# Layer 0's input projections of a two-layer decoder trunk, all with stationary activations and turned on TensorE afterwards

## The chip, the cores and the metric

The kernel runs on one core of a Trainium2 chip, in one launch. The metric is the device time in microseconds (us) from start to end of that core. Three runs of the kernel before gave 2135.3, 2136.2 and 2136.23 us; the median is 2136.2.

## What is computed

The trunk takes 256 tokens of 2048 features through two layers. Layer 0 is a recurrent mixer and a squared-ReLU MLP, layer 1 a dilated attention and an MLP. Only the mixer of layer 0 is touched by the change. Its reference, cut to what matters:

```python
def recurrent_mixers(h, w_in, ...):
    proj = h @ w_in                                   # (256 x 2048) @ (2048 x 6144)
    x_lru, y_lru, q_h, f_h, v_h, g_h = jnp.split(proj, list(IN_SPLITS), axis=-1)   # 1024 columns each
    lru = rg_lru(causal_depthwise_conv(x_lru, conv_w, conv_b), w_a, b_a, w_i, b_i, lam)
    lru = lru * jax.nn.gelu(y_lru.astype(F32), approximate=True)
    hg = hgrn2(q_h, f_h, v_h, g_h, lower_bound, g_norm)   # 8 heads of 128; RMSNorm per head, SiLU(g) gate
    mixed = jnp.concatenate([lru, hg], axis=-1).astype(h.dtype)
    return mixed @ w_out
```

The output of each head is divided by the root of its mean square over the head's 128 columns, multiplied by a gain per column, and by g times sigmoid(g). The recurrence and the convolution run along the tokens.

## The kernel before

**Number format.** Every large product is made from two rounded parts. An activation and a weight are each split into `hi` (the value rounded to float32r) and `lo` (the rest), and hi·hi, hi·lo and lo·hi are added up in PSUM. A weight tile of 128 x 2048 (1 MB, a *unit*) is fetched by SP into `raw`; ScalarE makes `hi` from it (line 130) and VectorE makes `lo` (line 131). The class `Weights` does both, in steps of 1024 columns for the units of layer 0's projections. `fetch` is called from `unit` and keeps two to three units ahead; `raw`, `hi` and `lo` have three buffers each.

**Two layouts of a projection.** In one, features come out on the partitions and tokens along the free dimension: the weights are the stationary operand of TensorE, the activations move. `project` (line 381) makes one block of 128 columns so, from one unit. With `cross` it issues 16 matmuls of 512 moving columns and 16 of 256; with `direct` 48 of 256. Heads 0 to 3 and `lru_in` of blocks 0 to 3 use `cross`; heads 4 to 7, `lru_in` of blocks 4 to 7 and all eight `lru_out` use `direct`. In the other layout tokens come out on the partitions: the activations are stationary and the weights move. `tokens` (line 348) makes 512 columns so from four units, 24 matmuls of 512 moving columns in each unit, in two PSUM banks, one for each half of the 256 tokens. Only the values v used this (`tokens_group`, line 373), in two groups of 512 columns.

**The row norm.** The activations in `bufa` are not normalised: the factor per token, `rt`, is applied after the projection. In the tokens layout it is a scale per partition, which the ACTIVATE that empties the bank takes along. In the features layout it is a row, so `over_tokens` (line 328) turns it once into `rs` and `scaled` (line 454) multiplies by it after each projection.

**A head.** `hgrn` (line 474) projects q and f, computes sigmoids, and then runs the scores in eight levels of doubling chunk size. In each level TensorE makes two small products of 64 columns from `qk` (line 509), VectorE copies masked results into `st` (line 512), and VectorE multiplies `qk` by a factor (line 526) before the next level's products. Three products with v give `po` (lines 533 to 535). The mean square and its inverse root are made for each head on its own (line 540 and `rsqrt`, 11 small VectorE operations); the two halves are scaled and turned to features (lines 544 and 547, `T.transpose`), the gate g is projected, and the product is split into `bufb` (block 8 + head).

**The other group.** `lru_in` projects a block of x, convolves it along the tokens and splits it into `bufb`. `lru_gates` multiplies four blocks by the gate weights (48 matmuls of 256) and computes sigmoids, then tanh and exp, then square roots, and runs the recurrence into `xc`. `lru_out` projects y, takes gelu, multiplies by `xc` and splits into `bufb` (blocks 0 to 7).

**Activation tables.** `lut` (line 251) keeps functions of one table together: whenever the kind changes (sigmoid; tanh and exp; square root), every later call is ordered behind all calls of the kind before.

**Order.** The string `ORDER` names the steps, and `units` follows it. Before, a head and a block of x alternate, v's second group comes in the middle, then gates 0, y 0 to 3, gates 1, y 4 to 7. After that `out_project` multiplies `bufb` by `w_out`: its first 512 columns take four units in the order `kgs` = (2, 3, 0, 1), which need blocks 8 to 11, 12 to 15, then blocks 0, 2, 4, 6 and at last 1, 3, 5, 7. All matmuls made through `mm` are chained in the order in which they are written. The small products of `hgrn` and the transposes are outside this chain: a scheduler puts each instruction into its engine's queue by priority, which is the place in the program moved ahead by `urgent` (400 instructions) or `stream` (150), and by when its operands are ready in the scheduler's own time model. On the chip each queue runs in that order.

`tokens` can run other work between its units: it takes the next entry of the list `steps` after each unit. Layer 1's attention uses this.

Of the kernel before, what the change touches and what calls it, by code (L numbers as in the profile page):

```python
# [10 lines left out]
F32 = mybir.dt.float32  # L11
# [30 lines left out]
def trunk_kernel(ctx, tc, head, x, xtok, cols, tab, masks, pos, fin, w_in, w_gate, w_out, w_qkv, w_o, w1, w2, out):  # L42
# [54 lines left out]
    where = {"x": (w_in, lambda i: i, 1), "y": (w_in, lambda i: 8 + i, 1), "g": (w_gate, lambda i: i, 1),  # L97
             "v": (w_in, lambda i: 14 + 16 * i, 4), "h": (w_in, lambda i: 18 + i // 4 * 16 + i % 4 * 3, 3)}
# [38 lines left out]
    def fetch():  # L137
        u = at[0]
        if u >= len(units):
            return  # L140
        at[0] += 1
        src, i = units[u][:2]
        with stream():
            if len(units[u]) > 2:
                combine(u, *units[u])
                return
            r = wraw.tile([P, 2048], F32, name="raw")
            loads[:] = [after(nc.sync.dma_start(r, src[i]), [])]
            made[u] = Weights(r, 1024)
# [107 lines left out]
    def cross(p, w, jobs, parts="hl"):  # L257
        for part in parts:
            for blk, mov, first, last in jobs:
                h, l = w.part(blk * P, P)  # L260
                if part == "h":
                    mm(p, h, mov, start=first, stop=False, skip_group_check=True)
                else:
                    mm(p[:, S:], l, mov[:, :S], start=False, stop=last, skip_group_check=True)

# [7 lines left out]

    PAIRWISE = 4
    of_head = lambda i: cross if i < PAIRWISE else direct
    YA = direct
# [51 lines left out]
    def over_tokens(r, turn=lambda o, i: T.transpose(o, i, ident)):  # L328
        p = psc.tile([P, 512], F32, name="pt", bufs=1)
        for j in range(2):  # L330
            turn(p[:, j * P:j * P + P], r[:, j:j + 1].to_broadcast([P, P]))
        return p[:, :S]

# [39 lines left out]
    def tokens_group(src, i0, rt=None, by_k=False, kgs=(0, 1, 2, 3), behind=()):  # L373
        ps = tokens(src, i0, bufa, kgs, by_k)
        v = vgs.tile([P, 2, 512], F32, name="vg")
# [5 lines left out]
    def project(src, i, mov, acc=None):  # L381
        w = unit(src, i)
        p = pmm.tile([P, 512], F32, name="p")
        jobs = [(k, mov[:, k], k == 0, k == KB - 1) for k in range(KB)]
        (acc or cross)(p, w, jobs)
        return p

# [7 lines left out]

    def square(j):
        q = wk.tile([P, 4, S], F32, name="gr", bufs=1).rearrange("p m s -> p (m s)").bitcast(BF16)
# [3 lines left out]
    vfirst = tokens_group(w_in, 14, by_k=True, behind=halfs[1:])  # L401
# [9 lines left out]
    rs = tmp.tile([P, S], F32, name="nr", bufs=1)  # L411
    A.copy(rs, over_tokens(rt))
# [41 lines left out]
    def scaled(p, z, acc=None):  # L454
        with urgent():
            if acc is direct:
                V.tensor_tensor(z, p[:, :S], rs, OP.mult)  # L457
            else:
                t = wk.tile([P, S], F32, name="t1", bufs=2)
                A.copy(t, p[:, S:])  # L460
                V.tensor_tensor(z, p[:, :S], t, OP.add)
                V.tensor_tensor(z, z, rs, OP.mult)

    def normed(p, name, bufs=2, acc=None):
        z = wk.tile([P, S], F32, name=name, bufs=bufs)
        scaled(p, z, acc)
        return z


# [4 lines left out]
    def hgrn(hd, vg):  # L474
        u0 = 18 + (hd // 4) * 16 + (hd % 4) * 3
        HA = of_head(hd)
# [3 lines left out]
        p = project(w_in, u0, bufa, HA)  # L480
        z = normed(p, "hz", 4, HA)
        lut(qp, z, AF.Sigmoid)
        V.scalar_tensor_tensor(qp, z, oml, qp, op0=OP.mult, op1=OP.mult)
        p = project(w_in, u0 + 1, bufa, HA)
        z = normed(p, "hz", 4, HA)
        f = wk.tile([P, S], F32, name="f", bufs=3)
        lut(f, z, AF.Sigmoid)
        lut(kq, z, AF.Sigmoid, scale=-1.0)
        V.tensor_scalar(f, f, oml, lb[:, hd:hd + 1], op0=OP.mult, op1=OP.add)
# [41 lines left out]
        vs = slice((hd % 4) * P, (hd % 4) * P + P)  # L531
# [4 lines left out]
        o = wk.tile([P, 2, P], F32, name="ho", bufs=2)  # L536
        hs = wk.tile([P, 2], F32, name="hs", bufs=2)
        for j in range(2):
            A.activation(o[:, j], po[:, j], AF.Square, accum_out=hs[:, j:j + 1])
        V.tensor_scalar(hs, hs, 1.0 / P, EPS, op0=OP.mult, op1=OP.add)  # L540
        hr = wk.tile([P, 2], F32, name="hr", bufs=2)
        rsqrt(hr, hs, 2)
        for j in range(2):
            A.activation(o[:, j], po[:, j], AF.Copy, scale=hr[:, j:j + 1])
        pt = psc.tile([P, 2, P], F32, name="pt", bufs=1)
        for j in range(2):
            T.transpose(pt[:, j], o[:, j], ident)
        p = project(w_in, u0 + 2, bufa, HA)
        z = normed(p, "hz", 4, HA)
        g = wk.tile([P, S], F32, name="g", bufs=2)  # L550
        lut(g, z, AF.Sigmoid)
        V.scalar_tensor_tensor(g, z, col("gn", hd), g, op0=OP.mult, op1=OP.mult)
        V.tensor_tensor(g, pt.rearrange("p j c -> p (j c)"), g, OP.mult)
        split_to(bufb[:, 8 + hd], g)
# [3 lines left out]
    def lru_in(b):  # L558
        XA = of_head(b)
        p = project(w_in, b, bufa, XA)  # L560
        xp = wk.tile([P, S + 4], F32, name="xp", bufs=1)
        V.memset(xp[:, :4], 0.0)
        scaled(p, xp[:, 4:], XA)
        A.activation(xc[:, b], xp[:, 4:], AF.Identity, bias=col("conv_b", b), scale=col("conv_w", 24 + b))
        for i in range(3):
            V.scalar_tensor_tensor(xc[:, b], xp[:, 1 + i:1 + i + S], col("conv_w", 8 * i + b), xc[:, b],
                                   op0=OP.mult, op1=OP.add)
        split_to(bufb[:, b], xc[:, b])

    def lru_gates(gp):  # L570
        w = unit(w_gate, gp)
        gr = wk.tile([P, 4, S], F32, name="gr", bufs=1)
        gi = wk.tile([P, 4, S], F32, name="gi", bufs=1)
# [21 lines left out]
    def lru_out(b):  # L595
        p = project(w_in, 8 + b, bufa, YA)
        y = tmp.tile([P, S], F32, name="z")
        scaled(p, y, YA)
        q = wk.tile([P, S], F32, name="q", bufs=1)
        A.activation(q, y, AF.Square, scale=math.sqrt(0.044715))  # L600
        V.scalar_tensor_tensor(q, q, 1.0, y, op0=OP.add, op1=OP.mult)
        lut(q, q, AF.Sigmoid, scale=2.0 * math.sqrt(2.0 / math.pi))
        V.tensor_tensor(y, y, q, OP.mult)
        V.tensor_tensor(y, y, xc[:, b], OP.mult)
# [627 lines left out]
```

## Time and profile before

| | us |
|---|---|
| median of three runs | 2136.2 |
| the profiled execution, its own time | 2134.95 |
| its span, first to last instruction | 2133.1 |
| of it, before `w_in`'s second step starts | 29 |
| the rest of layer 0's input projections and mixers | about 300 |
| `w_out` and all that follows | about 1804 |

In the profile PE is TensorE's matmuls, PEld its weight loads, DVE VectorE, ACT ScalarE, POOL GpSimd, SP the engine that issues most DMAs. A name such as `p<-bufa,hi` tells the tile that is written and those that are read. Views by line give a count, the busy time and the mean duration; a matmul's duration is that of one going through the pipeline, and since they overlap, what one costs in a row of many is read from the distance between starts in the timeline.

### The profile page before, as it was taken

What the parts mean: (1) busy time and instruction counts of PE and PEld (TensorE: products, weight loads), DVE (VectorE), ACT (ScalarE), POOL (GpSimd) and SP (SyncE); (2) the same over time, 40 slices, a digit from 0 to 9 for tenths busy, and PEclk for the clock granted to TensorE, in tenths of its full rate; (3) what the DMA queues carried; (4) which work ended last, traced back from release to release, by engine and by line L of the source; (5) the groups of instructions that cost most, each with busy time, mean ns of one, the idle gap of its engine ahead of it and who ended that gap; (6) DMA issues with size and microseconds to landing.
All of it is one profiled execution on the core that took longest, in us unless ns stands there. A gap on an engine that the chain in (4) does not pass through costs nothing.

```text
span 2133.1 us, 26563 instructions
## 1 busy us (share of the span) xinstructions
PE 2120.6 (99%) x10496; PEld 1796.1 (84%) x10496; DVE 1820.0 (85%) x1971; ACT 1306.2 (61%) x1394; POOL 72.3 (3%) x89
## 2 busy tenths in 40 slices
PE   9999999999999999999999999999999999999998
PEld 8889998888888888888888888888888888888887
DVE  7767789988888888889998888798988987988897
ACT  7444485666566566557665656566755655755764
POOL 0000000000000000000000000000000000000000
PEclk9999999999999999999999999999999999999999
DMA  8544446688878778877788667567888778787884
GB/s 328 175 171 144 156 155 224 217 256 257 253 232 272 251 242 246 275 243 236 239 271 249 207 215 219 215 211 242 238 241 282 236 247 262 251 254 238 275 260 156
DMA packets 69884, 498.13 MB, mean 234 GB/s; under 512 B 7808, under 2 KB 8064, under 8 KB 10240
## 3 DMA queue, kind: packets, MB, share of 16 engines
q1 hardware_dynamic: 57600, 410.90, 51.4%
q0 software_dynamic: 11872, 84.94, 21.3%
q8 instruction: 82, 1.34, 0.2%
q10 hardware_dynamic: 288, 0.61, 0.1%
q14 instruction: 42, 0.34, 0.0%
HBM read 494.31 MB, written 2.10 MB: 233 GB/s over the span
## 4 chain that ended last, share of the span: by engine, by line
PE 96%; DVE 2%; ACT 1%; DMA 1%; issue 0%; SPq 0%; DVEq 0%
PE p L221 61%; PE pd L221 15%; PE po L221 14%; PE pl L224 2%; PE pt L221 2%; PE pl L509 1%; DVE lo L131 1%; PE pl L221 1%; ACT hi L130 0%; DMA raw<-in_w_qkv 0%; DMA both_in<-in_head 0%; PE pd L493 0%; ACT bufa L284 0%; ACT L252 0%; DVE xc L593 0%
## 5 line engine op out<-in xcount | busy, mean ns | idle before, releaser
L130 ACT CAST hi<-raw 128x2048 fp32r<-128x2048 f32 (+1 forms) x408 | 663.4, 1641 | 505.1 <-PE p L221 304.1
L131 DVE TENSOR_TENSOR lo<-raw,hi 128x2048 fp32r<-128x2048 f32 (+1 forms) x408 | 793.9, 1954 | 181.1 <-ACT hi L130 175.1
L221 PE MATMUL p<-hi,bufa 128*128 128x512 f32 x1360 | 437.8, 392 | 0.6 <-ACT bufa L284 0.6
L221 PE MATMUL p<-hi,bufb 128*128 128x512 f32 x1264 | 404.4, 390 | 0.0
L221 PEld LDWEIGHTS p<-hi,bufa 128*128 128x128 f32 x1360 | 255.2, 188 | 53.7 <-ACT bufa L284 0.8
L131 DVE TENSOR_TENSOR lo<-s,hi 128x2048 fp32r<-128x2048 f32 x120 | 274.2, 2285 | 11.5 <-ACT hi L130 9.5
L221 PEld LDWEIGHTS p<-hi,bufb 128*128 128x128 f32 x1264 | 237.3, 188 | 48.9
L221 PE MATMUL p<-lo,bufa 128*128 128x512 f32 x680 | 265.4, 390 | 1.3 <-DVE lo L131 1.2
L130 ACT CAST hi<-s 128x2048 fp32r<-128x2048 f32 x120 | 229.6, 1913 | 52.0 <-PE po L221 23.1
L221 PE MATMUL p<-lo,bufb 128*128 128x512 f32 x632 | 245.9, 389 | 0.0
L221 PE MATMUL p<-bufa,hi 128*128 128x256 f32 (+1 forms) x1024 | 207.3, 313 | 0.1
L221 PEld LDWEIGHTS p<-bufa,hi 128*128 128x128 f32 x1024 | 166.6, 190 | 9.0 <-DVE hz L457 0.3
L221 PEld LDWEIGHTS p<-lo,bufa 128*128 128x128 f32 x680 | 127.7, 188 | 28.6 <-DVE lo L131 2.5
L221 PE MATMUL p<-bufa,lo 128*128 128x256 f32 x640 | 145.9, 286 | 0.0
L221 PEld LDWEIGHTS p<-lo,bufb 128*128 128x128 f32 x632 | 118.7, 188 | 24.4
L221 PE MATMUL pd<-hi,bufa 128*128 128x512 f32 x352 | 116.6, 393 | 0.0
L221 PE MATMUL p<-hi,formx 128*128 128x512 f32 x352 | 116.3, 391 | 0.0
L221 PEld LDWEIGHTS p<-bufa,lo 128*128 128x128 f32 x640 | 106.9, 191 | 1.3
L131 DVE TENSOR_TENSOR lo<-t,hi 128x2048 fp32r<-128x2048 f32 x40 | 91.5, 2288 | 16.5 <-ACT hi L130 16.5
L221 PE MATMUL po<-hi,bufb 128*128 128x512 f32 (+1 forms) x320 | 102.3, 386 | 0.0
L221 PE MATMUL p<-hi,formh 128*128 128x512 f32 x288 | 94.5, 389 | 0.0
L159 DVE TENSOR_TENSOR s<-s,raw 128x2048 f32<-128x2048 f32 x40 | 91.3, 2284 | 3.2 <-DMA raw<-in_w_qkv 3.1
(327 smaller groups left out, 3170.1 us busy)
## 6 DMA issues: line engine op xcount, KB each, us to landing
raw<-in_w SPq DMA_DIRECT2D x224, 1024.0 KB, 6.5
raw<-in_w_in SPq DMA_DIRECT2D x45, 1024.0 KB, 4.9
raw<-in_w_qkv SPq DMA_DIRECT2D x42, 1024.0 KB, 6.7
t<-in_w SPq DMA_DIRECT2D x32, 1024.0 KB, 6.6
t<-in_w POOLq DMA_DIRECT2D x32, 1024.0 KB, 8.8
s<-in_w POOLq DMA_DIRECT2D x32, 1024.0 KB, 8.7
raw<-in_w_out SPq DMA_DIRECT2D x15, 1024.0 KB, 4.9
raw<-in_w_o SPq DMA_DIRECT2D x15, 1024.0 KB, 4.9
```

What stands on the lines that cost most here:

```text
L130: casts[:] = [after(A.copy(h, w), [])]
L131: i = V.tensor_tensor(l, w, h.bitcast(F32), OP.subtract)
L159: return V.tensor_tensor(held[to], held[x], held[y], OP.add)
L221: chain[:] = [after(T.matmul(*args, **kw), chain)]
L224: chain[:] = [after(T.transpose(out_, in_, ident), chain)]
L509: T.matmul(pl[:, j], kq[:, js], halves(qp[:, js], c, True), start=True, stop=True)
```

## The change

All twelve groups of 512 columns of `w_in` now go through `tokens_group`. `project`, `cross`, `scaled`, `normed` and `over_tokens` are gone (`direct` stays for the gates), and so is the row `rs`; `rt` is applied by the ACTIVATE that empties each bank into a tile `tk` of 512 columns, of which there are seven buffers. Weights of `w_in` are laid out by groups and split in one step of 2048 columns.

Where features are needed on the partitions, the results are turned on TensorE: `turned` makes four 128 x 128 transposes into the one bank `pt`. A head turns its q and f; `lru_in` turns two blocks of x at a time and convolves straight from PSUM; `lru_out` turns two blocks of gelu(y) after `lru_gelu` has computed it on 512 columns; `finish` multiplies two heads' outputs by the inverse roots and by SiLU(g) with tokens on the partitions, turns them and splits them with the gain. The inverse roots are now made for four heads at once. One multiply-add of the forget gate moves from VectorE to ScalarE.

The order is new, and the heads and the other work are run between the units of later groups (`HOOKS`): a list of up to three entries for a group, one after each of its units. What is left after the last group, gelu and turning of y's second half, runs between the first two units of `w_out`, and the pool of the mixers is closed there too. The tiles of the gates, `gr` and `gi`, move into the room of `bufb`'s last quarter.

The diff, its core:

```diff
-    where = {"x": (w_in, lambda i: i, 1), "y": (w_in, lambda i: 8 + i, 1), ...
-    for step in ORDER.split():
-        src, first, n = where[step[0]]
-        units.extend((src, first(int(step[1])) + i) for i in range(n))
+    for g, step in enumerate(ORDER.split()):
+        if step[0] == "G":
+            units.append((w_gate, int(step[1])))
+        else:
+            units.extend((w_in, 4 * PLACE[step] + i) for i in range(4))
...
-            made[u] = Weights(r, 1024)
+            made[u] = Weights(r, 2048 if src is w_in else 1024)
...
+    def tokens_group(step, rt=None, by_k=False, behind=()):
+        steps[:] = HOOKS.get(step, ())
+        ps = tokens(w_in, 4 * PLACE[step], bufa, by_k=by_k)
+        v = vgs.tile([P, 2, 512], F32, name="tk", bufs=7)
...
+    def turned(tiles, at):
+        p = psc.tile([P, 2, S], F32, name="pt", bufs=1)
+        for i, (z, m) in enumerate(zip(tiles, at)):
+            for j in range(2):
+                T.transpose(p[:, i, j * P:j * P + P], z[:, j, m * P:m * P + P], ident)
+        return p
...
-        p = project(w_in, u0, bufa, HA)
-        z = normed(p, "hz", 4, HA)
-        lut(qp, z, AF.Sigmoid)
...
+        p = turned((done[f"q{g}"], done[f"f{g}"]), (at, at))
+        lut(qp, p[:, 0], AF.Sigmoid)
...
-        V.tensor_scalar(f, f, oml, lb[:, hd:hd + 1], op0=OP.mult, op1=OP.add)
+        A.activation(f, f, AF.Identity, scale=oml, bias=lb[:, hd:hd + 1])
...
+    def finish(g, half):
+        if not half:
+            hs = roots[g]
+            V.tensor_scalar(hs, hs, 1.0 / P, EPS, op0=OP.mult, op1=OP.add)
+            roots[g] = wk.tile([P, 8], F32, name="hr", bufs=2)
+            rsqrt(roots[g], hs, 8)
+        pair_ = [2 * half, 2 * half + 1]
+        for at in pair_:
+            o, z = outs[4 * g + at], done[f"g{g}"][:, :, at * P:at * P + P]
+            s = wk.tile([P, 2, P], F32, name="g", bufs=2)
+            lut(s, z, AF.Sigmoid)
+            V.tensor_tensor(s, s, z, OP.mult)
+            for j in range(2):
+                V.scalar_tensor_tensor(o[:, j], o[:, j], roots[g][:, 2 * at + j:2 * at + j + 1], s[:, j], ...)
+        p = turned([outs[4 * g + at] for at in pair_], (0, 0))
+        if g and not half:
+            bufb.tiles[3] = act.tile([P, 4, 2 * S], F32R, name="bufb3")
+        for i, at in enumerate(pair_):
+            split_to(bufb[:, 8 + 4 * g + at], p[:, i], col("gn", 4 * g + at))
...
+    def lru_gelu(n):
+        y = done[f"y{n}"]
+        q = outs[f"y{n}"] = vgs.tile([P, 2, 512], F32, name="tk", bufs=7)
+        for j in range(2):
+            A.activation(q[:, j], y[:, j], AF.Square, scale=math.sqrt(0.044715))
+            V.scalar_tensor_tensor(q[:, j], q[:, j], 1.0, y[:, j], op0=OP.add, op1=OP.mult)
+            lut(q[:, j], q[:, j], AF.Sigmoid, scale=2.0 * math.sqrt(2.0 / math.pi))
+            V.tensor_tensor(y[:, j], y[:, j], q[:, j], OP.mult)
+
+    def lru_out(n, half):
+        b0 = 4 * n + 2 * half
+        p = turned([done[f"y{n}"]] * 2, (2 * half, 2 * half + 1))
+        z = outs[f"y{n}"][:, half].rearrange("p (i s) -> p i s", i=2)
+        V.tensor_tensor(z, p, xc[:, b0:b0 + 2], OP.mult)
+        split_to(bufb[:, b0:b0 + 2], z)
+
+    HOOKS.update({
+        "q1": [head(0)], "f1": [head(1)], "v1": [head(2)], "x0": [head(3)],
+        "x1": [head(4), [do(lru_in, 0, 0)], [do(lru_in, 0, 1)]],
+        "g0": [head(5), [do(lru_in, 1, 0)], [do(lru_in, 1, 1)]],
+        "g1": [head(6), [do(finish, 0, 0)], [do(finish, 0, 1)]],
+        "y0": [head(7)],
+        "y1": [[do(lru_gelu, 0)], [do(lru_out, 0, 0), do(lru_out, 0, 1)], [do(finish, 1, 0)], [do(finish, 1, 1)]],
+    })
...
+    steps[:] = [[do(lru_gelu, 1)], [do(lru_out, 1, 0), do(lru_out, 1, 1), close_mixers]]
...
-ORDER = "v0 h0 x0 h1 x1 h2 x2 h3 x3 v1 h4 x4 h5 x5 h6 x6 h7 x7 g0 y0 y1 y2 y3 g1 y4 y5 y6 y7"
+ORDER = "v0 q0 f0 q1 f1 v1 x0 x1 G0 g0 g1 G1 y0 y1"
+PLACE = {step: n for n, step in enumerate(step for step in ORDER.split() if step[0] != "G")}
```

More of the change, by code (lines that the diff above doesn't have):

```diff
@@ L541, in hgrn @@
[L541 to L552, printed above, removed]
@@ L553, in hgrn @@
-        V.tensor_tensor(g, pt.rearrange("p j c -> p (j c)"), g, OP.mult)
-        split_to(bufb[:, 8 + hd], g)
-    xc = wk.tile([P, 8, S], F32, name="xc", bufs=1)
[L558 to L568, printed above, removed]
+            A.activation(o[:, j], po[:, j], AF.Square, accum_out=roots[g][:, 2 * at + j:2 * at + j + 1])
@@ L593, in lru_gates @@
             V.tensor_tensor_scan(xc[:, b], gr[:, m], xc[:, b], 0.0, op0=OP.mult, op1=OP.add)
[L595 to L604, printed above, removed]
-        split_to(bufb[:, b], y)
```

125 lines of the change are left out of this document (44 added, 81 removed).

## The prediction, made before the changed kernel was run

> **What bounds the kernel now.** I read the page first, then busy time by stage, then TensorE's groups of the first 460 us by shape, then the timeline.
>
> ```profile
> span 2133.1 us, 26563 instructions
> PE 2120.6 (99%) x10496; PEld 1796.1 (84%) x10496; DVE 1820.0 (85%) x1971; ACT 1306.2 (61%) x1394; POOL 72.3 (3%) x89
> ...
> PE 96%; DVE 2%; ACT 1%; DMA 1%; issue 0%; SPq 0%; DVEq 0%
> ```
>
> ```profile
> 29.00:135.00 106.00, 106.00 (x639) 94.43 (x638) 85.64 (x211) 57.64 (x103) 0.00 (x0) 1.00 0.57 201
> ...
> 160.00:329.00 169.00, 167.78 (x1411) 167.18 (x1411) 135.88 (x342) 101.41 (x202) 0.00 (x0) 1.00 0.43 150
> 329.00:350.00 21.00, 21.00 (x96) 17.39 (x95) 19.06 (x36) 11.32 (x17) 0.00 (x0) 1.00 0.75 270
> ```
>
> The chain that ended last is TensorE for 96% of the span. In the stages (columns: stretch, length, then busy time and count of PE, PEld, DVE, ACT, POOL, clock, DMA share, GB/s) it stays so in the part that the change touches, about 29 to 329 us: PE idles 1.22 us between 160 and 329, DVE is busy for 80% of each stretch, ACT for less, the DMA engines for half, and the granted clock is 1.00. What the change is worth is therefore what it takes from TensorE's queue, less what TensorE has to wait anew. Relief on DVE and ACT counts only where TensorE waits for them.
>
> **What a matmul costs in a row of many.** Starts in the timeline tell:
>
> ```profile
> 103.81 1.75 PE L221 MATMUL p<-bufa,hi 128*128 128x512 f32 x7
> 105.40 0.55 PE L509 MATMUL pl<-qk 128*128 128x64 f32 x4
> 105.77 1.18 PE L221 MATMUL p<-bufa,hi 128*128 128x512 f32 x4
> 106.78 2.06 PE L221 MATMUL p<-bufa,lo 128*128 128x256 f32 x16
> ```
>
> ```profile
> 205.26 0.40 PE L221 MATMUL p<-bufa,hi 128*128 128x256 f32 x2
> ...
> 208.49 0.40 PE L221 MATMUL p<-bufa,hi 128*128 128x256 f32 x2
> ```
>
> ```profile
> 330.95 0.62 PE L221 MATMUL p<-hi,bufb 128*128 128x512 f32 x2
> ...
> 337.75 0.62 PE L221 MATMUL p<-hi,bufb 128*128 128x512 f32 x2
> ```
>
> From 205.26 to 208.49 us lie nine groups of three matmuls of 256 columns: 3.23/27 = 0.1196 us each. From 330.95 to 337.75 lie ten groups of three of 512, in the tokens layout: 6.80/30 = 0.2267 us. The features layout costs the same for 512: 1.59/7 = 0.227 before the small products at 105.40. So twice the columns cost 1.90 times the time: each matmul carries some 12 ns beside its columns (2 x 0.1196 - 0.2267).
>
> **The main matmuls.** The counts:
>
> ```profile
> L221 PE MATMUL p<-bufa,lo 128*128 128x256 f32 x640 | 145.9, 286 | 0.0
> L221 PE MATMUL p<-bufa,hi 128*128 128x256 f32 x768 | 144.1, 287 | 0.1
> L221 PE MATMUL p<-bufa,hi 128*128 128x512 f32 x256 | 63.2, 394 | 0.0
> ```
>
> 768 = 24 `direct` units of 32, and 640 = 24 x 16 + 16 x 16 makes 16 `cross` units. A `direct` unit costs 48 x 0.1196 = 5.74 us, a `cross` unit 16 x (0.2267 + 0.1196) = 5.54, and a unit in the tokens layout 24 x 0.2267 = 5.44. The change saves 24 x 0.30 + 16 x 0.10 = **8.8 us**. v and the gates keep theirs.
>
> The Trainium skill, "TensorE: Matmul & The Clock Gate", section "Wait — 56ns, not 53.3ns?", speaks against so much: it gives about 2.5 ns of fixed cost to a matmul. By it the 24 x 24 + 16 x 8 = 704 matmuls that go would save 1.8 us, an estimate from that page, and the time below would be 7 us longer. The trace's own distances decide, so I keep 8.8 and give that rule no chance here.
>
> **The transposes.** A head, `finish`, `lru_in` and `lru_out` call `turned` 8 + 4 + 4 + 4 = 20 times, 80 transposes. These go:
>
> ```profile
> L547 PE MATMUL pt<-tab__183,ho 128*128 128x128 f32 x16 | 3.9, 272 | 0.0
> ...
> L328 PE MATMUL pt<-tab__183,nr 128*128 128x128 f32 x2 | 0.4, 272 | 0.0
> ```
>
> That leaves 62 more. Four transposes in a stream of 512s cost:
>
> ```profile
> 378.82 0.39 PE L221 MATMUL p<-hi,formh 128*128 128x512 f32 x1
> 379.05 0.60 PE L224 MATMUL pl<-tab__183,xall 128*128 128x128 f32 x4
> 379.41 0.48 PE L221 MATMUL p<-hi,bufb 128*128 128x512 f32 x1
> 379.72 0.40 PE L221 MATMUL p<-lo,bufb 128*128 128x512 f32 x1
> ```
>
> 378.82 to 379.72 is 0.90 us and holds two matmuls of 0.227, so four transposes cost 0.447 us, 0.112 each. The small products at 105.40 agree: 106.78 - 105.40 - 4 x 0.2267 = 0.47 for four. 62 x 0.112 = **6.9 us**. Low end: by columns alone, 12 ns and half of a 256's other 107, 0.066 us, the net is 80 x 0.066 - 18 x 0.066 = 4.1. High end: if none overlapped, 62 x 0.272 = 16.9. I take 6.9, because the row is this very operation among 512s. The heads' own small products (lines 493 to 535) stay as they are.
>
> TensorE's queue alone becomes 8.8 - 6.9 = **1.9 us shorter**.
>
> **What TensorE waits for anew.** DVE and ACT lose work: `scaled`, six of eight inverse roots, and a 2048-wide `lo` takes
>
> ```profile
> L131 DVE TENSOR_TENSOR lo<-raw,hi 128x2048 fp32r<-128x2048 f32 x67 | 153.4, 2289 | 37.9 <-ACT hi L130 37.8
> ...
> L804 DVE TENSOR_TENSOR y<-p,y 128x512 f32<-128x512 f32 x10 | 6.9, 688 | 4.0 <-PE p L221 4.0
> ```
>
> 2.29 us. They were hidden under TensorE, so this counts as nothing in mid-stage. In the opening a unit is now usable only after a whole 2048-wide cast and `lo`; its cover is the three units of `hi` and `lo`, and I charge nothing (up to 0.5). Three places are different, because a result that was spread over many units is now late by design.
>
> *`w_out`'s third unit.* It needs blocks 0, 2, 4, 6 in this order. Blocks 4 to 7 come from `lru_out`(1, ·), written behind `w_out`'s second unit, so its transposes stand in TensorE's queue behind that unit's matmuls and right ahead of the third's. Block 4 is wanted 6 x 0.2267 + 0.45 = 1.8 us later. Its path is transposes (0.45 and a pass of 0.27 less 0.11), a product from PSUM (0.69), a rounding on ACT (about the same), a difference on DVE (likewise): 2.7 us with every queue empty. The second half needs `pt` back, so it starts after the first's product and ends some 2 us later. With empty queues that stalls TensorE 0.6 to 1 us. They aren't empty: DVE was busy 19.06 of 21 us in this stretch, and the weights' casts and `lo`s, which run ahead by `stream`, and `mixed_forms` lie in between. Each of four DVE and two ACT steps can wait for a 1024-wide piece of about 1 us: 0 to 6 us, nothing if the scheduler found room for the transposes earlier. I take **4 us**, nearer to the top because DVE has 9% free.
>
> *`w_out`'s second unit* needs heads 4 to 7, and `finish`(1, 0) the roots of all four. Head 7 is written behind y0's first unit. In front of it stand the gates' square roots, since `lut` puts the head's sigmoids behind them:
>
> ```profile
> 307.84 0.47 ACT L252 ACTIVATE gi<-p,c__91 128x256 f32<-128x256 f32 x1
> ...
> 317.25 1.34 ACT L252 ACTIVATE gi<-gi 128x256 f32<-128x256 f32 x4
> ```
>
> From the last gate's sigmoid to the last root it took 10.8 us (with y's work on ACT between); y0's first unit covers 5.4, so the head starts up to 5 us late. A head takes, small products to `po`:
>
> ```profile
> 256.96 0.39 PE L493 MATMUL pd<-qk 128*128 128x128 f32 x2
> ...
> 294.53 0.39 PE L535 MATMUL po<-vg,st 128*128 128x128 f32 x2
> ```
>
> 38 us for head 7. With 3 us ahead of that and some 9 for `finish` (an estimate: twelve small DVE operations, products, transposes and splits, each behind a `lo`) it is ready 50 to 55 us after y0's first unit. TensorE gets there after eight units and some 60 small products: 43.5 + 6.7 = 50.2 us. 0 to 6 us, since a less busy DVE shortens the levels and the late start lengthens the whole; I take **2 us**, less than the middle for the emptier DVE. A stall here also gives the third unit's chain nothing, as that begins behind this unit.
>
> *Gates 0* want blocks 2 and 3 of x 5.4 + 24 x 0.1196 = 8.3 us after `lru_in`(0, 1) is written. Its path is transposes, two ACT steps, six convolution steps on DVE of about 0.5 us, a split: 5.6 us empty, up to 11 behind `lo`s and two heads. 0 to 3; I take **1 us**, as most of it fits.
>
> **The sum**: -8.8 + 6.9 + 4 + 2 + 1 = +5.1 us on the span of 2133.1. The median of the runs lies 3.1 above that span, so 2136.2 + 5.1 = **2141.3 us**.
>
> **The rivals.**
> *B, the covers hold.* The scheduler keeps TensorE's idle time as small as now (1.22 us), and only the queue counts: 2136.2 - 1.9 = 2134.3, not slower. For it: the same scheduler hid the tail of y before, with DVE just as full. Against: y's last block was wanted a unit later then, and no turn through TensorE stood in its path.
> *C, transposes don't overlap.* 16.9 in place of 6.9: 2151.3. The Trainium skill, same page, "Part 4: PE-mode transpose", gives about 275 ns to one in a kernel's context; its record here is 272, which agrees, but the distance between starts above is 0.112, and the clock stays at 1.00. Against it stand those rows; for it only that twenty bursts come in new company.
> *D, a head takes too long for its buffer.* The eighth `tk` tile is x1's, and it takes v0's room, which head 3 frees with `po`. Head 3 has seven units and 50 small products from where it is written, about 44 us. Head 2 took, with heads close together,
>
> ```profile
> 100.33 0.39 PE L493 MATMUL pd<-qk 128*128 128x128 f32 x2
> ...
> 164.08 0.39 PE L535 MATMUL po<-vg,st 128*128 128x128 f32 x2
> ```
>
> 64 us. From 44 us on x1's banks stay full and the gates stall: 20 us there, and again at `finish`: 2134.3 + 40 = 2174. Against: DVE was fuller, and a unit of v stood between.
> *E, cheap transposes and no waits.* 4.1 in place of 6.9, and the 1.22 idle gone: 2136.2 - 8.8 + 4.1 - 1.2 = 2130.3. For: a single transpose needs fewer columns. Against: the row of four.
>
> **How the numbers follow.** Forecast 0.45, B 0.27, C 0.06, D 0.09, E 0.13. 0.2% (4.3 us, 2131.9 to 2140.5) is about what a measurement can tell from no change. The forecast's own range is 2136 to 2149 (waits of 1 to 14 us); some 0.08 of its 0.45 lies within 0.2%. Faster: E, 0.13. Same: 0.27 + 0.08 = 0.35. Slower: 0.37 + 0.06 + 0.09 = 0.52. 2131 to 2150 leaves out D, C and half of E, 0.21.
>
> **What would show it.** Matmuls of 512 at 0.2267 us and four transposes at 0.45 show the queue; another distance breaks the first two terms. PE idle just ahead of `p<-hi,bufb` in `w_out`'s third unit, released by `bufb` on ACT or DVE, shows the 4; idle ahead of its second unit the 2; idle inside gates 0 the 1. If `w_out` starts about 2 us earlier than at 329.1 and runs without a gap, B holds and my waits are wrong. A bank of x1 emptied many us after its last matmul is D.

## The result, and the profile after

The changed kernel takes 2194.8 us (median of four runs, 2193.3 to 2196.2); the kernel before took 2136.2 on the same chip. The ratio is 1.0275, with a 95% interval of 1.0258 to 1.0293: 58.6 us slower, where the forecast was 5.1 slower and the range ended at 2150.

The page of the changed kernel, its span, busy times and granted clock:

```profile
span 2194.4 us, 25011 instructions
...
PE 2158.8 (98%) x9854; PEld 1784.0 (81%) x9854; DVE 1790.2 (82%) x1771; ACT 1312.4 (60%) x1337; POOL 72.5 (3%) x89
...
PEclk9999979999999999999999999999999999999999
```

642 matmuls and 200 VectorE instructions are gone, and yet TensorE is busy 38 us longer, and one slice of the clock row has a 7. The windows of the changed kernel (columns as in the prediction) tell where:

```profile
29.00:135.00 106.00, 106.00 (x494) 88.31 (x492) 57.25 (x86) 53.70 (x50) 0.00 (x0) 1.00 0.59 211
213.00:264.00 51.00, 51.00 (x258) 43.15 (x257) 42.75 (x91) 35.26 (x56) 0.00 (x0) 1.00 0.42 148
264.00:300.00 36.00, 22.98 (x96) 20.40 (x95) 15.07 (x42) 8.18 (x26) 0.00 (x0) 0.55 0.14 54
```

VectorE's share fell from 81% to 54% in the first stretch, as intended. From 264 to 300 us nothing is full: TensorE is busy for 23 of 36 us at a clock of 0.55, VectorE for 15, the DMA engines for a seventh. Everything waits for a chain there.

When `w_out`'s matmuls and all later ones are matched one by one in the two traces (7,724 of them), the changed kernel is 26.4 us late at the first, 46.1 after the 72nd (the end of `w_out`'s third unit), and then the lag grows evenly to 61.3 at the last. So there are three losses: before `w_out`, inside its first units, and a drift of 15 us over the untouched rest.

**The distances are those of the prediction.** TensorE in the changed kernel, four transposes between matmuls of 512:

```profile
126.18 0.39 PE L221 MATMUL p<-hi,bufa 128*128 128x512 f32 x1
126.41 0.60 PE L436 MATMUL pt<-tab__183,tk 128*128 128x128 f32 x4
...
127.31 0.63 PE L221 MATMUL p<-hi,bufa 128*128 128x512 f32 x2
...
129.36 0.61 PE L221 MATMUL p<-hi,bufa 128*128 128x512 f32 x2
```

From 126.18 to 127.31 lie three matmuls and four transposes: 1.13 - 3 x 0.227 = 0.45 us for the four. From 127.31 to 129.36 lie nine matmuls: 0.228 each.

**A head gets one level through per weight unit.** First TensorE's small products of one head (the two products of a level leave four records), then VectorE's queue at the same time (`lo` is the next unit's difference, lines 476 and 490 a level's copy and factor):

```profile
105.45 0.55 PE L473 MATMUL pl<-qk 128*128 128x64 f32 x4
111.83 0.55 PE L473 MATMUL pl<-qk 128*128 128x64 f32 x4
...
117.74 0.55 PE L473 MATMUL pl<-qk 128*128 128x64 f32 x4
124.11 0.55 PE L473 MATMUL pl<-qk 128*128 128x64 f32 x4
```

```profile
110.34 2.29 DVE L131 TENSOR_TENSOR lo<-raw,hi 128x2048 fp32r<-128x2048 f32 x1 [0.90 <-ACT hi L130]
112.55 0.29 DVE L476 COPY_PREDICATED st<-msk,pl 128x128 f32<-128x128 int8 x1
112.75 0.42 DVE L490 TENSOR_TENSOR qk<-qk,tot 128x256 f32<-128x256 f32 x1
...
116.71 2.29 DVE L131 TENSOR_TENSOR lo<-raw,hi 128x2048 fp32r<-128x2048 f32 x1 [2.88 <-ACT hi L130]
118.92 0.29 DVE L476 COPY_PREDICATED st<-msk,pl 128x128 f32<-128x128 int8 x1
```

The products of 111.83 us are copied at 112.55, as soon as `lo` lets VectorE go, and the factor is done at 113.17. The products of the next level come only at 117.74, 4.6 us later: in TensorE's queue they stand behind main matmuls, which follow each other without a gap. VectorE copies them at 118.92, behind the next unit's `lo`. Had the products come sooner, the copy would still have stood behind that `lo` in its queue, and the `lo` had waited 2.88 us, idle, for `hi`. ScalarE makes `hi` only when TensorE has freed a `hi` buffer, that is, once per unit; the cast had waited 4.45 us for that:

```profile
114.76 1.91 ACT L130 CAST hi<-raw 128x2048 fp32r<-128x2048 f32 x1 [4.45 <-PE p L221]
```

VectorE is not too full. Its queue and TensorE's each hold one level for each unit, and which of the two would give way first no run here separates. Eight levels at 6 us make a head of 44 to 50 us, and the heads go one after another: their `po` products come at 134.8, 178.6, 205.6, 240.6, 271.7, 285.8, 299.3 and 364.2 us, while the order writes a new one every 24 us.

**The backlog comes due at 264 us.** TensorE, once g1's matmuls are done:

```profile
277.05 1.08 PE L473 MATMUL pl<-qk 128*128 128x64 f32 x4 [0.88 <-DVE qk L490]
278.94 1.09 PE L473 MATMUL pl<-qk 128*128 128x64 f32 x4 [0.81 <-DVE qk L490]
...
299.89 0.64 PE L468 MATMUL pl<-qk 128*128 128x128 f32 x2
300.17 0.77 PE L221 MATMUL pl<-bufb,hi 128*128 128x256 f32 x2
```

With nothing else to do a level takes 1.9 us, at half the clock. Heads 4, 5 and 6 finish so, and the first matmul of gates 1, which writes a `pl` bank, follows head 6's last `pl` product at once.

**The tail.** TensorE in `w_out`'s second unit (first three rows) and third:

```profile
364.24 0.49 PE L497 MATMUL po<-tk,st 128*128 128x128 f32 x2 [1.11 <-ACT st L483]
369.54 1.26 PE L436 MATMUL pt<-tab__183,ho 128*128 128x128 f32 x4 [3.52 <-DVE ho L520]
371.37 0.79 PE L221 MATMUL p<-hi,bufb 128*128 128x512 f32 x1 [0.56 <-ACT bufb L271]
...
382.97 0.51 PE L221 MATMUL p<-hi,bufb 128*128 128x512 f32 x1 [0.34 <-ACT bufb L268]
385.10 0.74 PE L221 MATMUL p<-hi,bufb 128*128 128x512 f32 x2 [1.40 <-DVE bufb L269]
386.90 1.15 PE L221 MATMUL p<-hi,bufb 128*128 128x512 f32 x2 [0.83 <-DVE bufb L269]
```

Head 7 ends at 364 and its turn waits for `finish`; the second unit and its start lose 13 us. The third unit waits for blocks 4 to 7 just as foreseen.

**The drift.** The group of products with `formx`, of the kernel before and of the changed one:

```profile
L221 PE MATMUL p<-hi,formx 128*128 128x512 f32 x352 | 116.3, 391 | 0.0
```

```profile
L221 PE MATMUL p<-hi,formx 128*128 128x512 f32 x352 | 118.3, 397 | 0.0
```

The same instructions in layer 0's MLP and in layer 1, code that the change does not touch, take 6 ns longer, and the distance between the starts of two neighbours goes from 227.1 to 233.4 ns on the mean. Two things can be blamed: the two new 32 B temporaries of the inverse root for eight columns (`rs8`), which push `formx` and `formh` up by 64 B in SBUF, from 167456 and 200224 to 167520 and 200288; or another mix of traffic.

### The profile page after: what moved, and what is told of

The parts are those of the page before. It is cut to its first block, busy times and chain, and to the rows that moved or that the text cites. A ratio compares the mean times of both kernels' runs of the same rounds, so it can differ in the third digit from the quotient of the medians.

```text
span 2194.4 us, 25011 instructions
## 1 busy us (share of the span) xinstructions
PE 2158.8 (98%) x9854; PEld 1784.0 (81%) x9854; DVE 1790.2 (82%) x1771; ACT 1312.4 (60%) x1337; POOL 72.5 (3%) x89
## 4 chain that ended last, share of the span: by engine, by line
PE 96%; DVE 2%; ACT 1%; DMA 1%; issue 0%; SPq 0%; DVEq 0%
PE p L221 60%; PE pd L221 14%; PE po L221 14%; PE pl L224 2%; PE pt L221 2%; PE pl L473 1%; PE pl L221 1%; DVE lo L131 1%; ACT hi L130 0%; PE pt L436 0%; DMA raw<-in_w_qkv 0%; DMA both_in<-in_head 0%; PE po L497 0%; DVE qk L490 0%; PE pd L457 0%
## 5 line engine op out<-in xcount | busy, mean ns | idle before, releaser
L221 PE MATMUL p<-hi,bufa 128*128 128x512 f32 x2000 | 641.1, 393 | 0.8 <-ACT bufa L271 0.8
L221 PEld LDWEIGHTS p<-hi,bufa 128*128 128x128 f32 x2000 | 374.5, 188 | 78.6 <-ACT bufa L271 1.0
L221 PE MATMUL p<-hi,bufb 128*128 128x512 f32 x1264 | 409.7, 394 | 3.3 <-DVE bufb L269 2.2
L221 PE MATMUL p<-lo,bufa 128*128 128x512 f32 x1000 | 392.1, 392 | 1.3 <-DVE lo L131 1.3
L221 PEld LDWEIGHTS p<-lo,bufa 128*128 128x128 f32 x1000 | 187.9, 188 | 41.6 <-DVE lo L131 2.8
L159 DVE TENSOR_TENSOR s<-raw,t 128x2048 f32<-128x2048 f32 x40 | 91.3, 2283 | 0.4 <-DMA raw<-in_w_o 0.3
L221 PE MATMUL po<-hi,bufa 128*128 128x512 f32 x256 | 84.9, 392 | 0.0
L130 ACT CAST hi<-t 128x2048 fp32r<-128x2048 f32 x40 | 76.3, 1907 | 12.6 <-PE pd L221 6.4
L221 PE MATMUL pd<-hi,bufb 128*128 128x512 f32 x256 | 83.0, 389 | 0.0
```

Of the source, the lines that this page charges most:

```text
L130: casts[:] = [after(A.copy(h, w), [])]
L159: return V.tensor_tensor(held[to], held[x], held[y], OP.add)
L221: chain[:] = [after(T.matmul(*args, **kw), chain)]
```

## The experiments

Each was run beside the kernel before on the same chip; that one took 2135.3 to 2136.2 us. Labels with `a_` start from the changed kernel, with `b_` from the kernel before.

### Where formx and formh lie

```diff
  # in rsqrt: t = tmp.tile([P, n], F32, name=f"rs{n}", bufs=2)
  # a_pad
+ t = tmp.tile([P, 16 if n == 8 else n], F32, name=f"rs{n}", bufs=2)[:, :n]
  # a_fix
+ t = tmp.tile([P, 8], F32, name="rs2", bufs=2)[:, :n]
  # b_shift
+ t = tmp.tile([P, 16], F32, name=f"rs{n}", bufs=2)[:, :n]
  # b_512
+ t = tmp.tile([P, 72], F32, name=f"rs{n}", bufs=2)[:, :n]
  # b_480
+ t = tmp.tile([P, n], F32, name=f"rs{n}", bufs=17)
  # b_all0
  cst = pool("cst")
+ cst.tile([P, 120], F32, name="gap")
```

> The changed kernel with the two small tiles rs8 widened from 32 to 64 B, so that what is laid out behind them, formx and formh among it, moves by a further 64 B and comes to the place within 128 B that it had before the change. Nothing else differs. Address theory (a matmul whose stationary operand is formx or formh costs 233.5 ns in place of 226.6 because of the 64 B): those matmuls return to 226.6 ns and the time falls by some 15 us, to 2180. Rival (the longer distance comes from other engines' traffic or from the new order): no change, 2195.

> The kernel before with its two small tiles rs2 widened to 64 B each, which moves formx and formh by 64 B or a little more, and nothing else. Address theory: matmuls with formx or formh as the stationary operand go from 226.6 to about 233 ns and the time rises by some 15 us, to 2151. Rival (the order or the traffic): 2136, no change.

a_pad took 2194.6, no change. b_shift took 2150.0: the kernel before becomes 0.67% slower (0.52 to 0.82%) by a move of 64 B alone, and its row of `formx` shows the 397 ns of the changed kernel:

```profile
L221 PE MATMUL p<-hi,formx 128*128 128x512 f32 x352 | 118.3, 397 | 0.0
```

So the address does it, but not by its place within 128 B, which a_pad had restored in vain.

> The changed kernel with the eight-column temporaries of the inverse root under the name and in the two rooms of the two-column ones, so that formx and formh start at exactly the addresses that they had before the change (167456 and 200224). Address theory: those matmuls go back to 226.6 ns, and the time falls by some 15 us, to 2180, with the idle stretches of 200 to 390 us unchanged. Rival (the 64 B widening that had the same pitch of 233 was no test, since the place within 128 B is not what counts, and neither is the address): 2195, no change.

> The kernel before with formx and formh moved up by 512 B (167968 and 200736), by wider temporaries of the inverse root. 64 B up cost 14 us; in the changed kernel 128 B up of the old place cost the same as 64 B. If what counts is the place within 512 B, which is what one row of a 128-column operand takes: 226.6 ns a matmul and 2136. If it is the absolute place (a boundary above the old address): 233 ns and 2150.

a_fix took 2179.4, 15.4 less than the changed kernel: the drift is gone (43.9 us late after `w_out`'s third unit, 44.1 at the last matmul). b_512 (a single run, as b_480 and b_all0 below) took 2135.0, with the old duration:

```profile
L221 PE MATMUL p<-hi,formx 128*128 128x512 f32 x352 | 116.3, 391 | 0.0
```

> The kernel before with formx and formh moved by 480 B to 167936 and 200704, which are multiples of 512; so far places of 32 B past a multiple of 512 cost 226.6 ns a matmul and places of 96 and 160 B past it 233.5. If 32 B or less past it is harmless: 2135 and 226.6 ns. If only the offset that the other buffers share (32 B) is: 2150 and 233 ns.

> The kernel before with one gap of 480 B ahead of everything, so that all big tiles (activations, hi and lo of the weights, formx, formh) start at multiples of 512 instead of 32 B past one. In the kernel before all of them stand 32 B past a multiple of 512; moving formx and formh alone to a multiple of 512 cost 12 us. If what counts is that the stationary operand and the moving one (hi, lo) stand at the same place within 512 B: 2135, all at 226.6 ns. If 32 B is good by itself and 0 is bad: all of some 7700 matmuls of 512 columns take 6.8 ns more, 2185.

Moved alone to a multiple of 512, the two tiles are slow again, 2147.9 us (b_480); with every large tile at a multiple of 512 they are fast, 2136.3 us (b_all0). Rows of b_480 and of b_all0, where one more line of code makes line 221 line 222:

```profile
L221 PE MATMUL p<-hi,formx 128*128 128x512 f32 x352 | 118.0, 396 | 0.0
```

```profile
L222 PE MATMUL p<-hi,formx 128*128 128x512 f32 x352 | 116.3, 391 | 0.0
```

No place is good or bad by itself. A product is fast where its stationary tile stands at the same offset within 512 B as the other large tiles (32 B in the kernel before, 0 in b_all0). Its moving operand, `hi` or `lo`, is the natural partner, but the runs moved all other tiles together and do not single it out.

### What holds the heads

```diff
  # a_nopl: gates 1
- p = psc.tile([P, 512], F32, name="pl", bufs=2) if gp and not gate else pmm.tile([P, 512], F32, name="p")
+ p = pmm.tile([P, 512], F32, name="p")
  # a_half: in hgrn, behind a level's copies
+ if c == 8:
+     c = 128
+     continue
  # a_1024
- made[u] = Weights(r, 2048 if src is w_in else 1024)
+ made[u] = Weights(r, 1024)
```

> The changed kernel, but the second gates unit takes only pmm banks and never the pl bank that the heads' levels use. Theory that the pl bank holds it back (its first matmul waits for every earlier head's levels): the matmuls of gates 1 start right behind g1's last one, near 264 us, and TensorE's idle 264 to 300 us goes from there; but the heads' backlog stays and shows again ahead of w_out's second unit, so of the 24 us lost there only 0 to 12 are won: 2183 to 2195. Rival (gates 1 waits for another thing, its input blocks or a pmm bank): no change, 2195, and the idle stays where it is.

2184.3 us. The windows of a_nopl:

```profile
250.00:300.00 50.00, 49.95 (x277) 43.20 (x276) 41.59 (x95) 37.92 (x64) 0.00 (x0) 1.00 0.47 165
300.00:355.00 55.00, 45.10 (x212) 37.99 (x210) 30.26 (x54) 21.47 (x47) 0.00 (x0) 0.81 0.34 119
```

The idle stretch of 264 to 300 us is gone, gates 1 start at 264.5 right behind g1, and `w_out` starts at 322.9, 6 us before the kernel before. But the backlog waits behind it: heads 6 and 7 end at 338 and 351 us, `w_out`'s second unit stands for them, and of a stretch of 36 us only 10.5 are won. The `pl` bank decided where the backlog fell due, not that there was one.

> Each head leaves out its levels of 16, 32 and 64 columns: scores between blocks of those sizes and their factors are missing from the output. Backlog theory (a head gets about one level through per weight unit, because DVE serves each level behind the next unit's lo, so that the heads take 44 us each where a group supplies one every 24): heads end some 16 us sooner each, the idle of TensorE at 264 to 300 us vanishes and so does most of that at 361 to 390 us; 24 small products of 3 levels x 2 x 8 = 48 go besides, about 4 us. The time falls by 30 to 45 us, to 2150 to 2165. Rival (the idle is set by the gates' own chain and by lru_out, not by the heads): only the products go, 2188 to 2192.

2167.0 us: 28 less, where 30 to 45 were expected. The heads' `po` come at 117, 142, 168, 192, 207, 260, 273 and 330 us, and `w_out` starts at 327.5. Not all of the 28 is backlog: the records of the small products fall from 224 to 128, 24 levels of four, and at the 0.47 us for four that the prediction read they alone are worth up to 11 us, not the 4 that were expected. The rival, corrected by that, would have stood at 2184, still far from the result. What is left, besides the address's 15, are waits that have little to do with levels: 2.0 us at gates 0 for blocks of x, 3.0 ahead of head 6's first products for a sigmoid, and 4.6 ahead of the turn of head 7's outputs.

> The changed kernel with the input weights split in two casts and two lo of 1024 columns each, as before the change, and not in one of 2048. Theory that a level waits because DVE's queue alternates levels and units: the queue still has one level for each unit, so no change within 4 us of 2195. Rival (the 2.29 us lo of 2048 columns is what a level waits for): levels fit between the two pieces, heads go twice as fast, and 20 to 30 us go: 2165 to 2175.

2188.6 us, 6 less than the changed kernel: two us outside what the first theory gave, and far from its rival. VectorE's queue still has one level for each unit (copies at 105.49, 111.48 and 117.84 us, each behind its pair of `lo`). The width of the split is not what a level waits for.

### Two levels per unit

Each head becomes a generator that yields after a level, and two heads take turns. Both versions have a_fix's temporaries and a_nopl's banks.

```diff
+            yield                          # in hgrn, at the end of a level
+    def pair_of(h):
+        live = [hgrn(h), hgrn(h + 1)]
+        while live:
+            for f in list(live):
+                if next(f, live) is live:
+                    live.remove(f)
  # a_levels
-        "q1": [head(0)], "f1": [head(1)], "v1": [head(2)], "x0": [head(3)],
+        "q1": [[heads(0)]], "v1": [[heads(2)]], "x0": [[], [], [], [heads(4)]],
...
+        "g1": [[do(finish, 0, 0)], [do(finish, 0, 1)], [heads(6)]],
  # a_pairs
-ORDER = "v0 q0 f0 q1 f1 v1 x0 x1 G0 g0 g1 G1 y0 y1"
+ORDER = "v0 q0 f0 q1 f1 v1 x0 x1 g0 G0 g1 G1 y0 y1"
+        "g0": [[do(lru_in, 1, 0)], [do(lru_in, 1, 1)], [heads(6)]],
```

> The changed kernel at the old addresses (2179.4) with heads written in pairs, level by level in turn, and gates 1 in the pmm banks only; its order of groups and its gates stay. Heads 6 and 7 are written behind finish of the first four. Theory that one level per unit made the backlog: heads 0 to 5 end 30 to 60 us earlier than in the changed kernel, the idle of 264 to 300 us goes, that at the end stays for the late heads 6 and 7: 2155 to 2168. Rival (the gates and their own chain hold up TensorE there): 2175 to 2180.

2156.2 us. TensorE's small products in a_levels:

```profile
106.05 1.00 PE L473 MATMUL pl<-qk 128*128 128x64 f32 x8
111.95 1.00 PE L473 MATMUL pl<-qk 128*128 128x64 f32 x8
```

The pace is the same 6 us, now for two levels. Heads 0 to 5 end at 137, 150, 191, 203, 225 and 238 us in place of up to 286; heads 1, 3, 4 and 5 gain 29 to 48 us, head 2 gains 15 and head 0 nothing, so "30 to 60" was too much for some. `w_out` starts at 326.4, and the late heads 6 and 7 cost 24 us behind it, as expected.

> The changed kernel with its heads written in pairs, level by level in turn, so that two levels stand between one weight unit's lo and the next instead of one; heads 6 and 7 before finish (with eight ho tiles, and fewer f and g tiles for the room), gates 0 behind g0, gates 1 in the pmm banks only, and formx and formh at their old addresses. Nothing is left out. Theory that one level per unit made the backlog: heads end 44 us a pair, TensorE's idle before w_out falls from some 30 us to under 4, the clock stays at 1.00, w_out starts at 326 to 330 us, and with 0 to 8 us at the tail the time is 2132 to 2142. Rival (the heads are slow because DVE and ACT are too full, however they are written): two levels take two units, the idle stays, 2165 to 2180.

2153.1 us: between the theories. The heads are out of the way (the last `po` at 316 us), but `w_out` starts at 336.6. Gates 0, moved behind g0, now run into gates 1: gates 1 write into the room that gates 0's scans still read, and TensorE idles some 7 us between 265 and 284. And 8.6 us go in `w_out`'s second and third units, where heads are late no more: this is the tail that the prediction charged with 2 + 4.

### The order

The pairs of heads, `lru_in`, `finish` and `lru_out` are hooked in behind the units that finish their inputs, some units ahead of their use; q0 is now the first group, so that heads start four units earlier, and gates have other groups between them.

```diff
  # a_order
+ORDER = "q0 f0 v0 x0 q1 G0 f1 v1 x1 g0 G1 y0 y1 g1"
-    units.extend((w_out, 4 * n + g) for n in range(2) for g in (2, 3, 0, 1))
+    units.extend((w_out, 4 * n + g) for n in range(2) for g in range(4))
  # a_order2
+ORDER = "q0 f0 v0 x0 q1 f1 G0 v1 x1 g0 y0 G1 y1 g1"
+    with urgent():
+        finish(1, 0)
+        finish(1, 1)
  # a_order3
+ORDER = "q0 f0 v0 x0 q1 f1 G0 v1 x1 g0 y0 y1 G1 g1"
  # a_order4: as a_order2, but
-        "g0": [[go(6, 5), do(lru_in, 1, 0)], [do(lru_in, 1, 1)], [], [do(root, 0)]],
+        "g0": [[do(lru_in, 1, 0), go(6, 5)], [do(lru_in, 1, 1)], [], [do(root, 0)]],
```

> All of it put together, nothing left out: groups in the order q0 f0 v0 x0 q1 G0 f1 v1 x1 g0 G1 y0 y1 g1, heads in pairs level by level, gates 1 in the pmm banks, old addresses, and w_out's units in the order 0 1 2 3, so that the blocks of lru_out and finish are each wanted several units after they are written. Theory that the change itself is worth its shorter queue (1.9 us) once the waits that came with its order are gone: TensorE's idle up to the end of w_out's first 512 columns is under 4 us, the clock is 1.00, and the time is 2132 to 2140. Rival (the gates' chains on ACT and DVE find no room beside the heads whatever the order): 2145 to 2155, as with the pairs alone.

> As the version with the new order (2145.2), nothing left out, with these moves: each pair of heads is written some units earlier, G0 behind f1 and G1 behind y0, the inverse roots ahead of finish, finish of the last four ahead of w_out, and its second half and that of lru_out turned through a pl bank instead of waiting for pt. Theory that only the order's waits keep the change from its 1.9 us: the waits at gates 0 (1.6 us), gates 1 (3.4) and in w_out's last unit (5) fall to 0 to 4 together, 2134 to 2140. Rival (each wait taken away comes back one step further): 2142 to 2148.

> As the second version with the new order (2139.4), but gates 1 behind y1 instead of y0, so that the last pair of heads has its levels behind it when gates 1 begin; nothing left out. TensorE lost some 4 us there (small products one at a time and a stretch at a lower clock at 272 to 280 us). Theory: that goes, and lru_out of blocks 4 to 7 has one unit of cover less before w_out, 0 to 2 us: 2134 to 2138. Rival (it comes back ahead of w_out): 2139 to 2142.

> As the second version with the new order (2139.4), but the first block pair of lru_in for gates 1 written ahead of the last pair of heads; nothing left out. Theory: gates 1 have their input blocks earlier and the heads' last levels fall among the matmuls behind them: 2134 to 2138. Rival (the heads are then later for w_out's last unit): 2139 to 2144.

2145.2, 2139.4, 2137.4 and 2136.4 us. a_order lost 9 us at gates 0, gates 1 and in `w_out`'s last unit; a_order2 lost 4 at gates 1 alone; the last two have no wait of note left up to the end of `w_out`. a_order4 against the kernel before: 1.0004, interval 0.9995 to 1.0013, a tie, with 2135.3 beside it. No version beats the kernel before. The windows of a_order4:

```profile
160.00:327.00 167.00, 166.59 (x881) 142.43 (x880) 120.79 (x228) 105.82 (x177) 0.00 (x0) 1.00 0.46 160
327.00:350.00 23.00, 23.00 (x107) 18.99 (x106) 19.58 (x38) 13.67 (x22) 0.00 (x0) 1.00 0.61 224
```

TensorE is full at full clock. `w_out` starts at 326.4, 2.7 us before the kernel before, and from its third unit up to 1075 us the lead is an even 1.8. Then it is given back in layer 1. The longest waits of VectorE for a transfer between 1115 and 1145 us in the kernel before, and between 1125 and 1145 in a_order4:

```profile
DVE s L159 <- DMA raw<-in_w_qkv: 1.6, 1, 1.6
```

```profile
DVE s L159 <- DMA raw<-in_w_qkv: 3.1, 1, 3.1
```

A weight of layer 1 lands late there in both; TensorE waits for its `lo` 1.0 and 2.5 us, and in a_order4 the clock falls to 0.91 in that window. Why it is longer there stays open: TensorE waited 2.4 to 2.8 us at this place in a_half, a_levels, a_order2 and a_order3 too, some of which came there later than the kernel before and some sooner, and 0.9 to 1.4 in all other versions.

## Why the prediction was wrong, and where it was right

Taken against the kernel before of each run, the 58.6 us come apart so: the address 15.3 (changed kernel to a_fix), levels and bank 22.7 (a_fix to a_levels), order 19.5 (a_levels to a_order4), and 1.1 left. No run has the heads in turn without the change of the bank, so the 22.7 stay together.

**Main matmuls -8.8 and transposes +6.9: right in kind.** Both distances were measured again (0.228 and 0.45 for four), and in a_order4, where the waits are gone, the lead is 1.8 us where 1.9 was forecast for TensorE's queue. That they meet so closely is partly luck: 0.8 us of the lead is idle time that the kernel before has between 160 us and `w_out` and a_order4 has not (1.22 and 0.41 us in the windows), which leaves 1.0 for the queue. By the Trainium skill's 2.5 ns for a matmul's fixed cost ("TensorE: Matmul & The Clock Gate", section "Wait — 56ns, not 53.3ns?"), which the prediction set aside, the queue of that version would be some 5 us longer at this point (an estimate from that page's figure, 6.9 less 1.8); the trace has it shorter.

**The step that failed** is the list of waits. It named "Three places", charged nothing for heads that fall behind in the middle of the stage, and relied on "a less busy DVE shortens the levels". The heads were costed as small products only, "stay as they are". But a head is a chain of eight turns between TensorE and VectorE, and the two queues let one turn through per weight unit, 6 us, however little else VectorE has to do: its share fell from 81% to 54%, and the levels did not get shorter. In the kernel before, the first seven levels of head 7, from 264.49 to 285.87 us, follow each other every 3.6 us on the mean:

```profile
264.49 0.56 PE L509 MATMUL pl<-qk 128*128 128x64 f32 x4
...
268.02 0.56 PE L509 MATMUL pl<-qk 128*128 128x64 f32 x4
...
285.87 0.56 PE L509 MATMUL pl<-qk 128*128 128x64 f32 x4
```

So the pace of 6 us is not that of the head itself; since a_1024 rules out the width of the split, the new order of the queues is what is left for it. What came of it is a TensorE that is busy for 23 of the 36 us from 264 to 300, and 13 us lost at `w_out`'s second unit. The row of head 2 in rival D, 64 us, and 38 us for head 7 were in the prediction; eight heads one behind another at 44 us are 350 us, more than the 250 between the first pair q0, f0 and `w_out`. This sum was not made. (It is an upper one: where TensorE waited, around 204 us and from 264 us on, a level took 1.5 to 2 us, and the heads caught up.) Rival D had the right observation and the wrong victim: it let the head hold a `tk` buffer, so that banks would stay full, but 21 of the 24 copies out of the banks waited for TensorE to fill them; what the heads held were `pl`, `pt` and in the end `w_out`'s blocks. Its 2174 came nearest, at a chance of 0.09.

**The waits.** *`w_out`'s third unit*, 4 us: right. From its first transposes at 380.2 to its end at 391.6 it took 11.4 us, 5.1 more than its 24 matmuls and eight transposes, and the waits end with `bufb` on ACT and DVE as said; 2.6 of it are idle time, the rest goes with a lower clock. *Its second unit*, 2 us: right place, 13 in size, since head 7 came after seven late heads and not after one late start. *Gates 0*, 1 us: right mechanism, some 5 in size. TensorE in the changed kernel, and then VectorE's last step of `lru_in`(0, 1):

```profile
200.80 0.28 PE L221 MATMUL p<-bufb,lo 128*128 128x256 f32 x1
202.62 1.02 PE L473 MATMUL pl<-qk 128*128 128x64 f32 x4 [1.54 <-DVE qk L490]
...
208.95 0.56 PE L221 MATMUL p<-bufb,hi 128*128 128x256 f32 x1
```

```profile
208.25 0.68 DVE L269 TENSOR_TENSOR bufb<-xc,bufb 128x512 fp32r<-128x512 f32 x1
```

The stretch from 200.80 to 208.95 holds some 24 small products besides, worth 2.7 us at their pace in a row. The path of `lru_in` from its transposes at 196.55 to the end of the split took 12.4 us against "5.6 us empty, up to 11". Where these terms were priced, TensorE's lower clock during and after a wait was left out: 0.50 from 204 to 208 us, and 0.55 on the mean from 264 to 300.

**Not in the prediction at all** was the address: the roots "made for four heads at once" were counted as relief, and their two temporaries cost more than all the arithmetic of the change.

**Rival B**, 2134.3 with all covers held, is what a_order4 comes near (2136.4, a tie with the 2135.3 beside it), after two changes to the heads and a new order that the change did not have.

## What to carry to other kernels

When a long queue gets shorter, ask of each chain beside it how many turns it takes and which queue sets the pace of one turn: work that is "hidden" by hundreds of us in busy time can still be late, because its pace, here, is one step per buffer of the main stream. Two such chains taken in turn went through at the pace of one in a_levels. And compare the addresses of the large tiles before and after a change of small ones.

## What was not expected of the hardware

**Addresses.** Here a matmul of 512 columns starts 6.3 ns later on the mean (233.4 in place of 227.1) when its stationary tile lies at another offset within 512 B than the other large tiles; offsets of 64, 128 and 480 B from them were slow, 0 and 512 fast. The trace holds 1,280 matmuls of `hi` with `formx` or `formh` and half as many of `lo`, together 12.1 us, the greater part of the 13.9 and 15.4 that b_shift and a_fix showed, 0.7% of this kernel for 64 B. In b_shift the other matmuls of 512 columns, some 5,200 behind 420 us, start later too, 227.6 ns apart in place of 226.9, which adds some 3.6 us; in b_480 they do not (227.0). Why stays open.

**The clock falls without a long gap.** By the Trainium skill, "TensorE: Matmul & The Clock Gate", section "HAM oscillation — how this bites in real kernels", the rule is to leave TensorE no idle gap above some 3.4 us. The windows of the changed kernel, and TensorE's gaps in the second of the two places (that in the first is the 1.54 us at 202.62 above):

```profile
200.00:204.00 4.00, 2.10 (x12) 1.63 (x10) 3.94 (x9) 1.57 (x6) 0.00 (x0) 0.84 0.27 82
204.00:208.00 4.00, 3.50 (x15) 3.31 (x16) 2.73 (x11) 1.70 (x5) 0.00 (x0) 0.50 0.44 180
...
264.00:268.00 4.00, 1.21 (x9) 0.93 (x7) 3.40 (x10) 3.13 (x5) 0.00 (x0) 0.94 0.54 223
268.00:272.00 4.00, 2.08 (x9) 1.93 (x10) 2.72 (x6) 1.01 (x3) 0.00 (x0) 0.50 0.45 170
```

```profile
266.11 0.63 PE L473 MATMUL pl<-qk 128*128 128x64 f32 x4 [1.53 <-DVE qk L490]
269.57 1.08 PE L436 MATMUL pt<-tab__183,ho 128*128 128x128 f32 x4 [2.83 <-DVE bufb L272]
```

A mean of 0.84 over 4 us is 1.3 us at 0.50 and the rest at 1.00, so the clock fell near 202.7 us; 0.94 puts the second fall near 267.5. Ahead of the first stands one gap of 1.54 us, ahead of the second one of 1.53 and the first 0.8 us of another. The measurement decides: gaps of less than half the length that the rule names were enough here.
